# State-space parameters and x laid out on the host, loads in order of use, and TensorE in program order in the MLPs

## The chip, the cores and the metric

The kernel runs on one core of one Trainium2 chip. The metric is device time in microseconds (us); three runs of the kernel before gave 2289.91, 2291.15 and 2291.24, median 2291.15. The engines are TensorE (PE; its weight loads are PEld), VectorE (DVE), ScalarE (ACT), GpSimd (POOL) and SyncE (SP), which issues nearly all DMAs.

## The reference

A trunk of two layers over 256 tokens of width 2048, all in float32. Each layer mixes tokens in two ways at once, by differential attention (8 heads) and by a diagonal complex state-space model over 64 groups of 16 channels with 64 states each, and then runs a squared-ReLU MLP of width 8192:

```python
proj = x @ w_in[l]                      # 2048 x 4096: q, k, v, u
attn_out = diff_attention(q, k, v, lam, lam_init, attn_norm_g[l])
ssm_out = s5_mixer(u, lambda_re, lambda_im, log_dt, b_re, b_im, c_re, c_im, d, glu_w, glu_b)
mix = jnp.concatenate([attn_out, group_rms_norm(ssm_out)], axis=-1) @ w_out[l]
x = layer_norm(DEEPNORM_ALPHA * x + mix, ln1_g[l], ln1_b[l])
hid = jnp.square(jax.nn.relu(x @ w_up[l]))
x = layer_norm(DEEPNORM_ALPHA * x + hid @ w_down[l], ln2_g[l], ln2_b[l])

# s5_mixer, per group: discretize, scan over time, read out
dt = exp(log_dt); mag = exp(lr * dt); ab = mag * (cos(li * dt), sin(li * dt))
bb = f(ab, lr, li) * b                  # h[t] = ab * h[t-1] + bb @ u[t]
y = gelu(Re(c @ h) + d * u);  y = y * sigmoid(y @ glu_w + glu_b)
```

## The kernel before

Every matrix product runs in three passes on a split of both operands into a rounded part and a remainder (hi*hi, hi*lo, lo*hi), so that each weight tile that SP loads (`wfetch`, L179: 128x2x512, 512 KB, a "pair") is split by ACT (`wh`, L156) and DVE (`wl = w - wh`, L137). There are 6 buffers for raw pairs and 4 for split ones (`WS`, `WB`): the split of pair n waits until TensorE has done with pair n-4. `gemm_steps` (L216) makes one 128x512 product for both token tiles (t = 0, 1) with two accumulators `acc`; a step is one k tile of one token tile, 3 matmuls.

A layer has these stages. The mixer: eight products of 96 matmuls each from `xT` (k, u, u, q, v, v, k, q), with attention and the state-space work woven in. For the state space, `lay_params` (L356) turns the raw parameters into step factors (`ab`, `f`, powers `pw`), `base_b` and `base_c`; `half_prep` (L470) has POOL make `abc` and `fine` for half of the groups; `ssm_tables` (L489) has POOL make the table of powers in `ops` for one of eight blocks b; `ssm_turn` (L517) turns a block's `zx` on TensorE (`zT`, `pk`). Then per block: matmuls `X` (L598) from u, DVE work on `wk` with the table and a scan (L613), matmuls `Y` (L638). The two halves of X use two PSUM buffers, so the second waits until DVE has read the first. After the mixer come the output product with a layer norm (`last_chunk`), the MLP (16 blocks f: `up(f)`, 96 matmuls, then the product with `w_down` of block f-1, 96 matmuls), and a second `last_chunk`.

In the first layer x comes in rows (`load_x`), and TensorE turns it (`turn_x`, 32 transposes); the parameters come in their own layouts (`load_params`, L329, 17 DMAs) and are turned on TensorE too (L364, L365, and 16 transposes of `lc`, L246). For the second layer, `Ahead` (L554) does the state-space preparation during the first layer's MLP and spills the tables to DRAM.

What sets the order: SP's order is that of the program everywhere. In the mixer TensorE's order is fixed by a planner (`Flow`, L63): tasks wait for planned times (`L_LAY`, `L_HALF`, `L_TAB`, ...), and a step of a product advances the plan's clock by 0.68. `last_chunk` is written by hand. All else, and in the MLP TensorE as well, is put in order by the compiler's scheduler. Each engine then runs its list strictly in order.

Of the kernel before, what the change touches and what calls it, by code (L numbers as in the profile page):

```python
# [45 lines left out]
L_LOAD = 9.0  # L46
# [16 lines left out]
class Flow:  # L63
# [53 lines left out]
def trunk(ctx: ExitStack, tc: tile.TileContext, x, w_in, lambda_q1, lambda_k1, lambda_q2, lambda_k2,  # L117
          attn_norm_g, ssm_lambda_re, ssm_lambda_im, ssm_log_dt, ssm_b_re, ssm_b_im, ssm_c_re, ssm_c_im,
          ssm_d, glu_w, glu_b, ssm_norm_g, w_out, ln1_g, ln1_b, w_up, w_down, ln2_g, ln2_b, out):
# [112 lines left out]
    def gemm(*a, **kw):  # L232
        acc = {}
        for _ in gemm_steps(*a, done=acc.__setitem__, **kw):
            pass
        return acc

# [91 lines left out]
    def load_params(l):  # L329
        raw = op_tile()[0:96, 0]  # L330
        SY.dma_start(out=raw[0:32], in_=ssm_lambda_re[l].rearrange("(q g) p -> q (g p)", g=2))
        SY.dma_start(out=raw[32:64], in_=ssm_lambda_im[l].rearrange("(q g) p -> q (g p)", g=2))
        ld = ssm.tile([96, 2], F32, tag="ld", name="ld")
        SY.dma_start(out=ld[64:96], in_=ssm_log_dt[l].rearrange("(q g) -> q g", g=2))
        vec = op_tile()[0:32, 0]
        for i, v in enumerate((attn_norm_g, ssm_norm_g)):
            SY.dma_start(out=vec[8 * i:8 * i + 8], in_=v[l].rearrange("(b p) -> b p", p=P))
        for j in range(LC):
            SY.dma_start(out=vec[16:32].rearrange("x (r j c) -> x r j c", r=2, j=LC)[:, :, j],
                         in_=ssm_d[l].rearrange("(x r c) -> x r c", r=2, c=32))  # L340
# [846 lines left out]
```

## Time and profile before

| | us |
|---|---|
| median of three runs | 2291.15 |
| the profiled execution | 2289.99 |
| its span, first to last instruction | 2288.2 |
| TensorE busy | 2191.5 (96%) |
| VectorE busy | 1511.2 (66%) |
| ScalarE busy | 1080.8 (47%) |
| GpSimd busy | 341.1 (15%) |

The core's mean granted clock was 0.985. By the trace the first layer's mixer and output product run to about 475 us, its MLP to 1143, the second layer's mixer and output product to 1591, its MLP to 2236. A TensorE that is busy by the profile may still be slowed: back-to-back 128x512 matmuls start 0.227 us apart at full clock although each is shown as 0.39 us long, so the distance of starts tells more than the busy share.

### The profile page before, as it was taken

The numbers are of one execution on the slowest core, as the hardware profiler recorded it, in microseconds if no ns is written. First come the engines' busy times: TensorE is split into PE (matmuls) and PEld (weight loads), VectorE is DVE, ScalarE is ACT, GpSimd is POOL, SyncE is SP. The second block draws the span as 40 slices with busy tenths as digits, with TensorE's granted clock in tenths as the row PEclk, the third lists the DMA queues.
The fourth block names the chain that finished last, engine by engine and source line by source line (L and its number), as shares of the span: only waits on it lengthen the run. The fifth ranks groups of instructions, "written<-read, shape, count | busy, mean of one in ns | idle before, by whom it ended". The sixth has DMA issues, their size and how long they took to land.

```text
span 2288.2 us, 28955 instructions
## 1 busy us (share of the span) xinstructions
PE 2191.5 (96%) x10772; PEld 1770.5 (77%) x10772; DVE 1511.2 (66%) x1906; ACT 1080.8 (47%) x1543; POOL 341.1 (15%) x528
## 2 busy tenths in 40 slices
PE   7889889999999899999999999999999999999997
PEld 5767667788888788888877767777888888888886
DVE  5686877865765555555586996877565565556557
ACT  4445555354554445544534454544444444444443
POOL 1875500000352432310000000000000000000001
PEclk9999999999999999999999999999999999999999
DMA  7434344576566566666665654565666666666664
GB/s 221 141 111 129 107 124 149 192 206 201 177 183 203 178 203 223 204 211 209 215 215 173 201 174 133 164 220 149 185 189 187 195 186 192 191 186 190 186 198 144
DMA packets 229357, 414.35 MB, mean 181 GB/s; under 512 B 38592, under 2 KB 38752, under 8 KB 227168
## 3 DMA queue, kind: packets, MB, share of 16 engines
q1 hardware_dynamic: 228352, 405.82, 57.7%
q10 hardware_dynamic: 864, 6.69, 0.8%
q8 instruction: 85, 1.39, 0.3%
q14 instruction: 56, 0.46, 0.1%
HBM read 401.44 MB, written 11.01 MB: 180 GB/s over the span
## 4 chain that ended last, share of the span: by engine, by line
PE 75%; DVE 11%; POOL 6%; issue 4%; ACT 3%; DMA 2%; SPq 0%; DVEq 0%; ACTq 0%; POOLq 0%
PE acc L211 68%; POOL tm L137 3%; DVE wk L137 3%; DVE wl L137 3%; PE tp L246 2%; PE acc L813 2%; DVE res L153 1%; ACT wh L156 1%; POOL ops L137 1%; DVE wk L613 1%; POOL abc L137 1%; PE Y L638 1%; DVE res L137 0%; PE X L598 0%; ACT ops L156 0%
## 5 line engine op out<-in xcount | busy, mean ns | idle before, releaser
L137 DVE TENSOR_TENSOR wl<-w,wh 128x1024 fp32r<-128x1024 f32 x714 | 883.5, 1240 | 614.2 <-ACT wh L156 599.3
L156 ACT ACTIVATE wh<-w 128x1024 fp32r<-128x1024 f32 x714 | 754.0, 1060 | 802.8 <-PE acc L211 751.0
L211 PE MATMUL acc<-wh,xTh 128*128 128x512 f32 x1440 | 567.0, 401 | 7.3 <-ACT wh L156 6.7
L211 PE MATMUL acc<-wl,xTh 128*128 128x512 f32 x1440 | 567.0, 394 | 2.4 <-DVE wl L137 2.4
L211 PE MATMUL acc<-wh,xTl 128*128 128x512 f32 x1440 | 566.6, 394 | 0.0
L211 PE MATMUL acc<-wh,hidh 128*128 128x512 f32 x1024 | 407.5, 398 | 1.4 <-ACT raw L156 1.0
L211 PE MATMUL acc<-wh,hidl 128*128 128x512 f32 x1024 | 400.0, 391 | 0.0
L211 PE MATMUL acc<-wl,hidh 128*128 128x512 f32 x1024 | 399.2, 390 | 0.0
L211 PEld LDWEIGHTS acc<-wh,xTh 128*128 128x128 f32 x1440 | 274.5, 191 | 71.2 <-ACT wh L156 8.0
L211 PEld LDWEIGHTS acc<-wh,xTl 128*128 128x128 f32 x1440 | 274.2, 190 | 58.2
L211 PEld LDWEIGHTS acc<-wl,xTh 128*128 128x128 f32 x1440 | 274.5, 191 | 57.6 <-DVE wl L137 3.8
L211 PEld LDWEIGHTS acc<-wh,hidl 128*128 128x128 f32 x1024 | 192.4, 188 | 41.4
L211 PEld LDWEIGHTS acc<-wh,hidh 128*128 128x128 f32 x1024 | 192.8, 188 | 40.0 <-ACT raw L156 1.3
L211 PEld LDWEIGHTS acc<-wl,hidh 128*128 128x128 f32 x1024 | 192.8, 188 | 37.6
L137 DVE TENSOR_TENSOR res<-res,acc 128x512 f32<-128x512 f32 x288 | 196.5, 682 | 18.6 <-PE acc L211 17.0
L294 POOL TENSOR_TENSOR rs<-rs,mhalf 128x1 f32<-128x1 f32 x8 | 7.8, 978 | 1047.3 <-DVE rs L150 1047.3
L137 POOL TENSOR_TENSOR tm<-ops,pw 128x64 f32<-128x64 f32 (+2 forms) x192 | 126.1, 678 | 26.9 <-ACT ops L156 20.6
L156 ACT ACTIVATE raw<-acc 128x512 f32<-128x512 f32 x80 | 47.1, 589 | 65.2 <-PE acc L211 65.1
L137 POOL TENSOR_TENSOR ops<-tm 128x64 f32<-128x64 f32 (+2 forms) x96 | 75.6, 788 | 7.1
L150 POOL TENSOR_SCALAR ss<-ss 128x2 f32<-128x2 f32 x16 | 4.3, 269 | 394.7 <-ACT sq L156 394.7
L137 DVE TENSOR_TENSOR hidl<-tp,hidh 128x512 fp32r<-128x512 f32 x64 | 44.0, 687 | 28.7 <-ACT hidh L156 28.7
L211 PE MATMUL acc<-wh,mAh 128*128 128x512 f32 x128 | 53.6, 418 | 1.8 <-DVE res L137 1.1
(179 smaller groups left out, 1981.2 us busy)
## 6 DMA issues: line engine op xcount, KB each, us to landing
w<-in_w_up SPq DMA_DIRECT2D x256, 512.0 KB, 4.5
w<-in_w_down SPq DMA_DIRECT2D x256, 512.0 KB, 4.7
w<-in_w_in SPq DMA_DIRECT2D x128, 512.0 KB, 4.2
w<-in_w_out SPq DMA_DIRECT2D x64, 512.0 KB, 4.1
spilled<-ops SPq DMA_DIRECT2D x8, 1088.0 KB, 7.8
w<-in_glu_w SPq DMA_DIRECT2D x16, 512.0 KB, 4.1
ops<-spilled ACTq DMA_DIRECT2D x6, 1088.0 KB, 6.2
gb<-in_ln_g SPq DMA_DIRECT2D x8, 512.0 KB, 8.1
```

Source lines behind the costliest of these rows:

```text
L137: (eng or V).tensor_tensor(out=out, in0=in0, in1=in1, op=op)
L150: (eng or V).tensor_scalar(out=out, in0=a, scalar1=s1, scalar2=s2, op0=op0, **kw)
L153: V.scalar_tensor_tensor(out=out, in0=a, scalar=s, in1=b, op0=op0, op1=op1)
L156: S.activation(out=out, in_=in_, func=func, **kw)
L211: TE.matmul(out=acc, lhsT=a[:, c], rhs=b, start=(first and i == 0), stop=(last and i == 2))
L246: TE.transpose(ps[:, i], src(i), ident)
L294: G.tensor_tensor(out=self.rs, in0=self.rs, in1=mhalf[:, 0:1], op=ALU.pow)
L613: V.tensor_tensor_scan(out=flat(h[:, i]), data0=flat(dec), data1=flat(s[:, i]), initial=0.0, op0=ALU.mult, op1=ALU.add)
L638: TE.matmul(out=d, lhsT=cx[:, 2 * i + ri, 2 * hf + r].rearrange("p g c -> p (g c)"), rhs=e, start=(i == 1 and ri == 0), stop=(ri == 1), sk ...
L813: TE.matmul(out=acc[t], lhsT=(lo if i == LH else hi)[:, c], rhs=(wl if i == HL else wh)[:, k % 2], start=seen[t] == 0, stop=seen[t] == 3 * ...
```

## The change

The host now gives x a second time, by channel (`x_t`), and the state-space parameters by state and channel (`vectors`, `b_t`, `c_t`, `lambdas`). x is split from SBUF by ACT and DVE in four groups of 512 channels, without TensorE; `load_params` makes 5 DMAs instead of 17; `lay_params` has one small transpose left (`dtT`). SP's order at the start: x group 0 in two halves, two pairs, the step sizes and `vectors`, x group 1, two pairs, `b_t`, `c_t`, `lambdas`, x group 2, two pairs, x group 3, the other pairs. The rows of x (`res`) are loaded after the first q product. In the first product the token tiles alternate every 4 k tiles, where they alternated every 8. In the plan of the first mixer, two waits (`L_LOAD`, `L_LAY`) go, and `L_LAY` is put ahead of the first half on the plan's account of POOL.

In the MLPs TensorE's order is now that of the program: the transposes of block f's `raw` come after steps 4 and 9 of `up(f+1)`, and the state-space preparation of the second layer is planned by one `Flow` over the whole MLP, one block f later than before.

```diff
+    def tick(self, dt):
+
+        self.now += dt
+        t = True
+        while t:
+            t = next((t for t in self.tasks if t[2]()), None)
+            if t:
+                t[2] = next(t[1], None)
+                if t[2] is None:
+                    self.tasks.remove(t)
...
     def load_params(l):
-        raw = op_tile()[0:96, 0]
-        SY.dma_start(out=raw[0:32], in_=ssm_lambda_re[l].rearrange("(q g) p -> q (g p)", g=2))
...
+
+        ld = sm.tile([32, 2], F32, tag="ld", name="ld", bufs=1)
+        SY.dma_start(out=ld, in_=log_dt[l])
+        prm = ssm.tile([P, 96], F32, tag="prmT", name="prm")
+        SY.dma_start(out=prm, in_=vectors[l])
         yield
-        lb = ssm.tile([P, 4, NP_, GC], F32, tag="wk", name="lb")
-        for a, v in enumerate((ssm_b_re, ssm_b_im)):
...
+        wk = ssm.tile([P, 4, NP_, GC], F32, tag="wk", name="lb")
+        SY.dma_start(out=wk[:, 0:2], in_=b_t[l])
+        yield
+        base_b, base_c = (tile4k([P, 2, NP_, GC], F32, "base") for _ in range(2))
+        SY.dma_start(out=base_c, in_=c_t[l])
+        yield
         lq = ssm.tile([P, 4, HD], F32, tag="abc", name="lq")
-        for i, v in enumerate((lambda_q1, lambda_k1, lambda_q2, lambda_k2)):
-            SY.dma_start(out=lq[:, i], in_=v[l].partition_broadcast(P))
-        return raw, ld, vec, lq, lb, lc
+        SY.dma_start(out=lq.rearrange("p i d -> p (i d)"), in_=lambdas[l].partition_broadcast(P))
+        return ld, prm, lq, wk, base_b, base_c
+
+    def loading_rest(gen, to):
+        to.append((yield from gen))
...
     def lay_params(fl, p, l, loaded):
-        raw, ld, vec, lq, lb, lc = loaded
-        G.tensor_tensor(out=ld[64:96], in0=ebase[64:96, 0:2], in1=ld[64:96], op=ALU.pow)
-        V.tensor_copy(out=raw[64:96].rearrange("q (g p) -> q g p", g=2),
-                      in_=ld[64:96].unsqueeze(2).to_broadcast([32, 2, 64]))
+        ld, prm, lq, wk, base_b, base_c = loaded
+        raw = op_tile()[0:32, 0]
+        G.tensor_tensor(out=ld, in0=ebase[0:32, 0:2], in1=ld, op=ALU.pow)
+        V.tensor_copy(out=raw.rearrange("q (g p) -> q g p", g=2), in_=ld.unsqueeze(2).to_broadcast([32, 2, 64]))
+        p["vec"] = sm.tile([P, 32], F32, tag="vecT", name="vecT")
+        V.tensor_copy(out=p["vec"], in_=prm[:, 64:96])
         yield fl.slot("tp", dt=L_PARAM)
         give = fl.take("tp")
-        ps = ps_t.tile([P, 4, P], F32, tag="tp", name="prmT_ps")
-        TE.transpose(ps[:, 0, 0:96], raw, ident[0:96, 0:96])
...
+        ps = ps_t.tile([P, 4, P], F32, tag="tp", name="dtT")
+        TE.transpose(ps[:, 0, 0:32], raw, ident[0:32, 0:32])
+        dt = sm.tile([P, 32], F32, tag="dtT", name="dtT", bufs=1)
+        V.tensor_copy(out=dt, in_=ps[:, 0, 0:32])
...
-        base_b, base_c = (tile4k([P, 2, NP_, GC], F32, "base") for _ in range(2))
-        t1 = lb[:, 2:4]
...
+        lb, t1 = wk[:, 0:2], wk[:, 2:4]
+        ts(base_c[:, 1], base_c[:, 1], -1.0, ALU.mult)
...
+        fl.pool = fl.now + L_LAY
...
-            if 0 <= f - 6 < 8:
-                fl = Flow(sx=2)
-                fl.add(0, ssm_turn(fl, *self.q[f - 6][0:2]))
-                fl.run()
+            if 0 <= f - 7 < 8:
+                self.fl.add(0, ssm_turn(self.fl, *self.q[f - 7][0:2]))
...
-            if 0 <= f - 4 < 8:
-                self.q[f - 4] = ssm_tables(fl, self.p, f - 4)
+            if 0 <= f - 5 < 8:
+                self.q[f - 5] = ssm_tables(fl, self.p, f - 5)
...
-    def load_x(t, n):
-        for h in range(n):
...
+    def load_x(g):
+        xr = tile4k([P, 4, T], F32, "xr")
+        for h in range(2 if g == 0 else 1):
+            k = slice(2 * h, 2 * h + 2) if g == 0 else slice(0, 4)
+            SY.dma_start(out=xr[:, k], in_=x_t[:, 4 * g + k.start:4 * g + k.stop])
+            act(xT.hi[g][:, k], xr[:, k])
+            sub(xT.lo[g][:, k], xr[:, k], xT.hi[g][:, k].bitcast(F32))
+
+
+    loading, loaded = load_params(0), []
+    load_x(0)
+    fetched.extend([wfetch(w_in[0], k, AW) for k in (0, 2)])
+    next(loading)
+    load_x(1)
+    fetched.extend([wfetch(w_in[0], k, AW) for k in (4, 6)])
+    for _ in loading_rest(loading, loaded):
+        pass
+    load_x(2)
+    fetched.extend([wfetch(w_in[0], k, AW) for k in (8, 10)])
+    load_x(3)
+    first = lambda done: gemm_steps(xT, w_in[0], KT, AW, done)
...
-                yield lambda: loaded
-                yield fl.after(L_LOAD)
                 yield from lay_params(fl, p, 0, loaded[0])
-                yield fl.after(L_LAY)
...
-            if l == 0:
-                for i, test in enumerate(kproj(0)):
...
+            yield from kproj(0)
             for i in range(2):
                 yield from uproj(i)
             yield from qproj(0)
+            if l == 0:
+                for t in range(NT):
+                    SY.dma_start(out=res[t], in_=x[t * P:(t + 1) * P])
...
-        def up(f):
-            if f == 0:
...
+        def up(f, between=()):
+
+            acc, at = {}, dict(between)
+            steps = first(acc.__setitem__) if f == 0 else gemm_steps(xT, w_up[l], KT, f * NB, acc.__setitem__)
+            for i, _ in enumerate(steps):
+                tick()
+                if i in at:
+                    at[i]()
             hh = Split("hid", 1)
+
+            def turn(t, raw):
+                ps = transpose4(lambda i: raw[:, i * P:(i + 1) * P])
+                hh.put(t, 0, ps)
+            turns = []
             for t in range(NT):
                 raw = rawp.tile([P, NB], F32, tag="raw", name="raw")
                 act(raw, acc[t], AF.Relu)
                 act(raw, raw, AF.Square)
-                ps = transpose4(lambda i: raw[:, i * P:(i + 1) * P])
-                hh.put(t, 0, ps)
...
+                turns.append(lambda t=t, raw=raw: turn(t, raw))
+            return hh, turns
+
+        tick = lambda: None
         if l + 1 < DEPTH:
             ahead = Ahead(l + 1)
-            params = ahead.p
-        for f in range(1, NF):
...
+            params, tick = ahead.p, lambda: ahead.fl.tick(0.68)
+        with tc.manual_schedule(engines={ENG.PE}):
+            prev, turns = up(0)
+            for f in range(1, NF):
+                cur, then = up(f, ((4, turns[0]), (9, turns[1])))
+                if l + 1 < DEPTH:
+                    ahead.between(f)
+                for nb in range(4):
+                    if f == NF - 1 and 0 < nb < 3:
+                        then[nb - 1]()
+                    done = lambda t, acc: add_partial(t, acc, nb, ALPHA if f == 1 else None)
+                    for _ in gemm_steps(prev, w_down[l], 4, nb * NB, done, kt0=4 * (f - 1)):
+                        tick()
+                prev, turns = cur, then
+                if l + 1 < DEPTH:
+                    ahead.after(f)
...
+    state = lambda name: get(name).reshape(DEPTH, NP_, P).transpose(0, 2, 1)
+    column = lambda name: get(name).reshape(DEPTH, 8, P).transpose(0, 2, 1)
+    x = get("x").reshape(T, D)
+    give("x", x)
+    give("x_t", x.reshape(T, KT, P).transpose(2, 1, 0))
+    give("w_in", get("w_in"))
+    give("lambdas", np.concatenate([get("lambda_" + n) for n in ("q1", "k1", "q2", "k2")], axis=1))
+    give("log_dt", get("ssm_log_dt").reshape(DEPTH, NP_, 2))
+    skip = np.broadcast_to(get("ssm_d").reshape(DEPTH, 16, 2, 1, 32), (DEPTH, 16, 2, LC, 32))
+    give("vectors", np.concatenate([state("ssm_lambda_re"), state("ssm_lambda_im"), column("attn_norm_g"),
+                                    column("ssm_norm_g"), skip.reshape(DEPTH, 16, P).transpose(0, 2, 1)], axis=2))
+    pairs = lambda n: get(n).reshape(DEPTH, NP_, 2, *get(n).shape[2:])
+    give("b_t", np.stack([pairs("ssm_b_" + n).transpose(0, 2, 3, 1, 4).reshape(DEPTH, P, NP_, GC)
+                          for n in ("re", "im")], axis=2))
```

On TensorE, at the start of the program (`res0`, `res1` are the rows of x, `acc` the first product's accumulators; the numbers tell buffers apart). Before:

```order
L246 MATMUL tp_127<-ident_87,res0_111 128x128 x4
L246 MATMUL tp_134<-ident_87,res0_111 128x128 x4
L246 MATMUL tp_141<-ident_87,res0_111 128x128 x4
L246 MATMUL tp_148<-ident_87,res0_111 128x128 x4
L211 MATMUL acc_178<-wh_157,xTh_115 128x512
L211 MATMUL acc_178<-wl_158,xTh_115 128x512
```

The same place now, from the tenth matmul on (nothing but matmuls of `acc_168` stands ahead):

```order
L220 MATMUL acc_168<-wh_174,xTh_115 128x512
L220 MATMUL acc_168<-wl_175,xTh_115 128x512
L220 MATMUL acc_168<-wh_174,xTl_119 128x512
L362 MATMUL dtT_197<-ident_87,ops_181 128x32
L220 MATMUL acc_169<-wh_170,xTh_115 128x512
L220 MATMUL acc_169<-wl_171,xTh_115 128x512
```

The 16 transposes ahead of the first matmul are gone, and so are the 16 of the second token tile after 12 matmuls; after 12 matmuls stands the transpose of the step sizes, and the second token tile follows with the same weights.

On VectorE, during the first products, where `base_b` is made (`lb` holds the raw b and products with `f`). Before, the two `base` rows stand behind the 13th and the 14th split (`wl`) of the program:

```order
L137 TENSOR_TENSOR lb<-lb,f 128x512
L137 TENSOR_TENSOR wl<-w,wh 128x1024
L137 TENSOR_TENSOR base<-lb 128x512
L137 TENSOR_TENSOR wl<-w,wh 128x1024
L137 TENSOR_TENSOR lb<-lb,f 128x512 x2
L137 TENSOR_TENSOR base<-lb 128x512
L137 TENSOR_TENSOR wl<-w,wh 128x1024 x6
```

Now they stand behind the 10th and the 12th:

```order
L146 TENSOR_TENSOR lb<-lb,f 128x512
L146 TENSOR_TENSOR base<-lb 128x512
L146 TENSOR_TENSOR wl<-w,wh 128x1024
L146 TENSOR_TENSOR lb<-lb,f 128x512 x2
L146 TENSOR_TENSOR wl<-w,wh 128x1024
L146 TENSOR_TENSOR base<-lb 128x512
L146 TENSOR_TENSOR wl<-w,wh 128x1024 x8
```

The second `base` row, for which POOL's first half waits, moved from behind 14 splits to behind 12.

On TensorE, in the first MLP, the turn of block 4 of the second layer's state space (`zT`). Before, it stands in the midst of the product with `w_down`, between two accumulators:

```order
L211 MATMUL acc_6724<-wl_6735,hidh_6186 128x512
L211 MATMUL acc_6724<-wh_6734,hidl_6187 128x512
L525 MATMUL zT_7766<-ident_87,zx_7189 128x128 x4
L211 MATMUL acc_6725<-wh_6728,hidh_6186 128x512
L211 MATMUL acc_6725<-wl_6729,hidh_6186 128x512
```

Now:

```order
L220 MATMUL acc_7954<-wl_7959,hidh_7567 128x512
L220 MATMUL acc_7954<-wh_7958,hidl_7568 128x512
L511 MATMUL zT_7971<-ident_87,zx_7377 128x128 x4
L521 MATMUL pk_7977<-ops_7375,zx_7377 32x32 x8
L220 MATMUL acc_7954<-wh_7958,hidh_7567 128x512
L220 MATMUL acc_7954<-wl_7959,hidh_7567 128x512
```

It moved from the end of block f = 7 to the start of the product with `w_down` of f = 11, with `pk` right behind it; the other seven turns stand at the same place of their blocks.

## Rows read from the trace of the kernel before

**Rows 1.** Busy time by stretch: first MLP and second, same start and end points.

```profile
475.69:1143.03 667.34, 660.27 (x3080) 541.74 (x3079) 391.46 (x440) 322.87 (x407) 150.39 (x229) 0.99 0.65 201
1591.02:2235.55 644.53, 644.53 (x2902) 533.48 (x2901) 370.82 (x376) 298.27 (x323) 0.00 (x0) 1.00 0.63 191
```

Its columns are the stretch, its length, busy us (and instructions) of PE, PEld, DVE, ACT and POOL, the granted clock, the busy share of the DMA engines, and GB/s.

**Rows 2.** The same view of the first mixer.

```profile
0.00:51.10 51.10, 36.42 (x149) 27.25 (x150) 25.02 (x48) 18.94 (x25) 8.48 (x26) 0.93 0.75 220
74.20:100.20 26.00, 19.79 (x110) 15.60 (x108) 10.14 (x12) 10.70 (x20) 23.15 (x50) 0.94 0.51 162
116.20:318.00 201.80, 178.26 (x1165) 134.42 (x1165) 160.55 (x227) 98.57 (x219) 104.85 (x162) 0.94 0.39 117
```

**Rows 3.** PE's waits in all: for whom; us, times, longest.

```profile
PE Y L638 <- DVE wk L137: 18.5, 22, 3.2
...
PE zT L525 <- ACT zx L156: 5.7, 1, 5.7
```

**Rows 4.** PE's order of time, first matmuls: start, us, what, [idle before <-releaser].

```profile
3.88 1.09 PE L246 MATMUL tp<-ident,res 128*128 128x128 f32 x4 [3.88 <-DMA res<-in_x]
...
10.16 0.79 PE L211 MATMUL acc<-wh,xTh 128*128 128x512 f32 x1 [1.22 <-ACT wh L156]
11.42 0.80 PE L211 MATMUL acc<-wl,xTh 128*128 128x512 f32 x1 [0.46 <-DVE wl L137]
...
12.44 0.63 PE L211 MATMUL acc<-wh,xTh 128*128 128x512 f32 x1
12.87 0.63 PE L211 MATMUL acc<-wl,xTh 128*128 128x512 f32 x1
...
15.40 0.40 PE L211 MATMUL acc<-wl,xTh 128*128 128x512 f32 x1
```

**Rows 5.** The same: the wait in the first product, and its 96th matmul.

```profile
37.62 0.80 PE L211 MATMUL acc<-wh,xTh 128*128 128x512 f32 x1 [5.25 <-ACT wh L156]
...
51.11 0.39 PE L211 MATMUL acc<-wh,xTl 128*128 128x512 f32 x1
```

**Rows 6.** ACT's order of time at the start: splits that waited for their load.

```profile
9.06 1.06 ACT L156 ACTIVATE wh<-w 128x1024 fp32r<-128x1024 f32 x1 [2.10 <-DMA w<-in_w_in]
...
14.50 1.06 ACT L156 ACTIVATE wh<-w 128x1024 fp32r<-128x1024 f32 x1 [2.47 <-DMA w<-in_w_in]
```

**Rows 7.** DMA issues: count, KB each, median us from issue to landing.

```profile
lq<-in_lambda_k SPq DMA_DIRECT2D x4, 32.0 KB, 6.2
```

**Rows 8.** DVE and POOL in order of time: `base_b`, first half's start, first table's end.

```profile
62.47 0.69 DVE L137 TENSOR_TENSOR base<-lb 128x512 f32<-128x512 f32 x1
...
63.24 1.54 POOL L137 TENSOR_TENSOR tm<-base,ab 128x256 f32<-128x256 f32 x1 [1.95 <-DVE base L137]
...
66.54 1.20 POOL L137 TENSOR_TENSOR tm<-base,ab 128x256 f32<-128x256 f32 x2
...
96.90 0.72 POOL L137 TENSOR_TENSOR ops<-tm 128x256 f32<-128x256 f32 x1
```

**Rows 9.** PE in order of time: the two halves of block 0's X.

```profile
88.84 0.71 PE L598 MATMUL X<-uT,ops 64*128 64x128 f32 x8
...
98.41 1.82 PE L598 MATMUL X<-uT,ops 64*128 64x128 f32 x8 [5.86 <-DVE wk L137]
```

**Rows 10.** Chain that ended last, in order of time: pieces of both MLPs (start, us).

```profile
875.60 2.95 PE acc L211 x12
...
921.41 2.95 PE acc L211 x12
...
1657.31 40.83 PE acc L211 x180
1701.79 40.83 PE acc L211 x180
```

**Rows 11.** PE in order of time, first MLP: its two longest waits.

```profile
629.30 0.50 PE L211 MATMUL acc<-wh,hidh 128*128 128x512 f32 x1 [1.04 <-ACT raw L156]
...
793.62 1.12 PE L525 MATMUL zT<-ident,zx 128*128 128x128 f32 x4 [5.68 <-ACT zx L156]
```

More of the change, by code (lines that the diff above doesn't have):

```diff
@@ L116, in trunk @@
 @with_exitstack
-def trunk(ctx: ExitStack, tc: tile.TileContext, x, w_in, lambda_q1, lambda_k1, lambda_q2, lambda_k2,
-          attn_norm_g, ssm_lambda_re, ssm_lambda_im, ssm_log_dt, ssm_b_re, ssm_b_im, ssm_c_re, ssm_c_im,
-          ssm_d, glu_w, glu_b, ssm_norm_g, w_out, ln1_g, ln1_b, w_up, w_down, ln2_g, ln2_b, out):
+def trunk(ctx: ExitStack, tc: tile.TileContext, x, x_t, w_in, lambdas, log_dt, vectors, b_t, c_t, glu_w, glu_b,
+          w_out, ln1_g, ln1_b, w_up, w_down, ln2_g, ln2_b, out):
     nc = tc.nc
@@ L230, in gemm_steps @@
                     yield
[L232 to L236, printed above, removed]
     def split_evac(ps, hi, lo):
@@ L557, in __init__ @@
             self.loading, self.p, self.q, self.l = load_params(l), {"spilled": []}, {}, l
+            self.fl = Flow(tp=2, sx=2)
         def between(self, f):
[L561 to L564 removed]
+            if 0 <= f - 7 < 8:
+                self.fl.add(0, ssm_turn(self.fl, *self.q[f - 7][0:2]))
         def after(self, f):
[L567 removed]
+            fl = self.fl
             if f < 3:
                 try:
[L570 removed]
+                    for _ in range(2):
                         next(self.loading)
@@ L733, in trunk @@
     xT = Split("xT", 4)
-    def load_x(t, n):
-        for h in range(n):
-            cs = slice(h * D // n, (h + 1) * D // n)
-            SY.dma_start(out=res[t][:, cs], in_=x[t * P:(t + 1) * P, cs])
-    def turn_x(t):
-        for g in range(4):
-            ps = transpose4(lambda i: res[t][:, (4 * g + i) * P:(4 * g + i + 1) * P])
-            xT.put(t, 4 * g, ps)
-    load_x(0, 4)
-    turn_x(0)
-    first_w = [wpair(w_in[0], k, AW) for k in (0, 2)]
-    load_x(1, 2)
-    first_w.append(wpair(w_in[0], 4, AW))
-    loading = load_params(0)
-    first = lambda done: gemm_steps(xT, w_in[0], KT, AW, done, apart=True, pre=first_w)
+    def load_x(g):
[17 more added lines that the diff above has]
+    first = lambda done: gemm_steps(xT, w_in[0], KT, AW, done)
     NF = FF // NB
@@ L1074, in main @@
         def main():
-            if l == 0:
-                for i, test in enumerate(kproj(0)):
-                    if i == 3:
-                        with tc.manual_schedule(engines={ENG.Activation, ENG.DVE}):
-                            turn_x(1)
-                            first_w.append(wpair(w_in[0], 6, AW))
-                            fetched.extend([wfetch(w_in[0], k, AW) for k in (8, 10)])
-                        fl.now += 1.76
-                        loaded.append((yield from steps(loading, 0.0)))
-                    yield test
-            else:
-                yield from kproj(0)
+            yield from kproj(0)
             for i in range(2):
```

76 lines of the change are left out of this document (11 added, 65 removed).

## The prediction, written before the changed kernel ran

> **What bounds the kernel now.** I read the busy time by stretch first, then TensorE's waits in total, then the stretches where it waits in order of time, and the chain of waits last. The second MLP has no idle time at all: 644.53 us long, 644.53 us of TensorE. The first MLP, with the same products between the same points, takes 667.34 [rows 1]. In the first mixer TensorE idles 14.7 of the first 51.1 us and 6.2 of the 26 from 74.2 on [rows 2]. So the kernel is bound by TensorE, and there is time to be had only where it waits: the start, the first state-space blocks, the first MLP. I price these three places against the profiled execution, 2289.99 us (span 2288.2), which lies 1.2 us below the median of the runs, 2291.15. One unit first: in the second MLP a piece of 180 matmuls takes 40.83 us, so matmuls at full clock start 0.227 us apart, and a block takes 1701.79 - 1657.31 = 44.48 us [rows 10].
>
> **The start, up to the first product's 96th matmul, at 51.11 us now [rows 5].** Before, TensorE's first instruction is a transpose at 3.88, and its first matmul starts at 10.16, 1.1 us after the first pair landed (9.06) and ACT began to split it [rows 4, 6]. By 9.06, 1 MB of x and 0.5 MB of weights are in; by 14.50 four more transfers of 0.5 MB, so one takes (14.50 - 9.06) / 4 = 1.36 us [rows 6]. In the new order 0.5 MB of x stands ahead of the first pair, not 1 MB: the pair lands at 7.7, the first matmul starts at 8.8, the second, which waits for DVE's remainder, 1.26 later as now [rows 4], at 10.1. At the low clock the starts are 0.43 apart (12.44, 12.87) [rows 4].
>
> How many matmuls run at the low level? Before, 16 transposes from 3.88 on and then 11 matmuls did, until the one at 15.40 [rows 4]. Now there are no transposes ahead. At the one end 11 matmuls run low again: the 96th comes at 10.1 + 10 x 0.43 + 85 x 0.227 + 0.3 for the transpose of the step sizes = 34.0. At the other, matmuls fill the 5.6 us of the transposes (3.88 to the first matmul, less its wait) at the low level too, 13 more, so all 24 of the first four k tiles: 10.1 + 24 x 0.43 + 72 x 0.227 + 0.3 = 37.0, which is 14.1 earlier than now. The trace has one rise after transposes and fits either; I take 37.0, the nearer to what the row shows as a stretch. The Trainium skill ("TensorE: Matmul & The Clock Gate", Part 4: PE-mode transpose) says that transposes don't count as TensorE activity the way matmuls do; by it the first end would hold, and the sum below would be 3.0 lower.
>
> Do loads keep up? At 1.36 us per 0.5 MB x group 1 is in at 10.4, pair 4 (of k tiles 6 and 7) at 13.1, `b_t` and `c_t` at 15.9, x group 2 at 17.3 plus what `lambdas` costs, the last pair at 24.1 plus that. TensorE wants group 2 at 37.0 - 48 x 0.227 = 26.1, less some 3.5 for its splitting by ACT and DVE (1.06 and 1.2 for one like it, and a wait in their lists): 22.6. `lambdas` is one DMA of 128 KB repeated over partitions. By its bytes it is 0.35 us; but four DMAs of 32 KB of the same kind took up to 6.2 us from issue to landing [rows 7]. So group 2 lands between 17.6 and 23.5, against 22.6. I take no wait, since one of 128 partitions' rows in place of four is nearer to the low end. If a wait comes it is like the one at 37.62, which cost 5.25 of idle time [rows 5] and a second stretch of low clock. That wait itself stands behind the loads of the parameters, 17 DMAs, and goes with them; what is late next is the clock. The 32 transposes of x and 18 of the parameters go too; they lie ahead of the 96th matmul and are in this difference already. Range of the term: -17.1 to -9; value -14.1.
>
> **The first blocks of the state space.** X's second half waits 5.86 us at 98.41 for DVE [rows 9], which waits for POOL's first table, finished at 96.90 + 0.72 = 97.62 [rows 8]. POOL's chain from `base_b` (63.24) to that is 34.4 us [rows 8]. Counted from the 96th matmul (51.11), `base_b` is ready at +12.1 and the table at +46.5. In the new order of VectorE the second `base_b` stands behind 12 splits; the twelfth needs the eighth pair's buffers, free at the 96th matmul, and then ACT's 1.06, its own 1.2 and the 0.69 of `base_b`: +3.0. The table comes at +37.4. TensorE reaches the first half of X at 88.84 - 51.11 = +37.7 now, 3 matmuls (0.7) later in the new order, and the second half 12 matmuls and the half's 0.7 after it: +41.9. So the table is 4.5 us early, and the second half comes at +41.9 in place of 98.41 - 51.11 = +47.3: -5.4 us. That needs `ab` and `f` by then; their inputs land at 16.5 or so and the chain behind them on ACT and DVE is some 20 instructions of 0.2 to 0.4, with splits of pairs between them, so it is done well ahead of the twelfth split.
>
> What stands against it is POOL's pace: the same instruction took 1.54 us right beside DVE's splits and 0.60 each in a pair of 1.20 without [rows 8]. The Trainium skill ("SBUF — State Buffer", Who interferes with whom) says why: a VectorE instruction with two SBUF inputs, as the split is, holds a read port that GpSimd needs. In the new order POOL's 34.4 us lie beside running products, a split every 12 matmuls (2.7 us), so 12 or 13, where about 10 ran before; 3 more of 1.2 us are 3.6, and the table is then 0.9 early instead of 4.5. The sum stays, and the rival on this chain below gets more chance. Bounds: 0 (the chain gains nothing) to -7 (with the low clock behind the wait). Behind Y of block 0 the matmuls stand at the same places to within 3, and 18.5 us of waits of Y for the scan [rows 3] stay; VectorE's order differs in places, which I put at 0, -5 to +5.
>
> **The first MLP.** It is 667.34 - 644.53 = 22.8 us longer than the second [rows 1]. What must stay is eight turns: a block with one turn takes 921.41 - 875.60 = 45.81, 1.33 over 44.48 [rows 10]; eight are 10.6. One `dtT` is 0.3. The rest, 11.9 us, goes: 16 transposes of `lc` and two of the parameters (about 2.3 with the breaks), the 5.68 us wait of `zT` for ACT at 793.62 with the low clock behind it (about 7.3), the 1.04 us at 629.30, and small ones [rows 3, 11]. The long wait was for `abc`, which POOL made only just before; now `zT` of block 4 stands at f = 11, and `abc` is made behind the table of block 3 during f = 8. With `pk` and `zT` in one piece a turn may cost less than 1.33; with 0.9 each the term is -15, and if order costs waits again -8. Value -11.9.
>
> **What costs nothing.** In the second MLP the transposes move, but none goes: 0. The rows of x are 2 MB more, 4 x 1.36 = 5.4 us of DMA time, behind weights that run 6 raw pairs (16 us) ahead; uncovered it would cost 5.4. ACT and DVE split x from SBUF in place of PSUM, same sizes.
>
> **Sum.** 2289.99 - 14.1 - 5.4 - 11.9 = 2258.6; with the 1.2 us to the median 2259.8. I predict 2259, with 2249 to 2266 for this case.
>
> **Rivals.** (1) The first product waits for x or weights as it does now: 5.3 us of idle time and 16 matmuls at low clock (3.2) put the 96th at 45.5, a gain of 5.6 in place of 14.1: 2268. For it: the loads of repeated rows [rows 7]; against: 17 DMAs of parameters became 5. (2) POOL's chain holds the mixer where it is: `ab` or `c_t` come late, POOL starts at 63 as now, and the second half of X stays at 98.4. Then only the MLP gains: 2279. For it: POOL's 1.54; against: 4.5 us of lead. (3) The fixed order in the first MLP does not do what it says: the wait for `zT` only moves, and the low clock with it. Then 8 or more of the 11.9 stay: 2268 to 2271. (4) Slower: with TensorE in fixed order, each of the 30 starts of a product with `w_down` waits for ACT to empty the accumulators that `up` has just filled, since ACT has splits queued ahead; the price is the wait of 1.04 us at 629.30 [rows 11], twice a block, since both accumulators are wanted: 30 x 2 x 1.04 = 62 us, so 2322. It decides the sign from 31.4 / 30 = 1.05 us a block on. Against it: 15 such starts in the second MLP cost nothing [rows 1].
>
> **Chances.** Forecast 63 in 100, (1) 14, (2) 8, (3) 6, (4) 5, and 4 for mishaps that cancel. What a measurement of this kernel can tell from no change is about 0.2%, 4.6 us. Faster: 63 + 14 + 8 + 6 = 91; same 4; slower 5. The range goes from 2246, all three terms and VectorE's order at their far ends (-17.1, -7, -15, -5), to 2276, which takes in (1) and (3) and the near ends (-9, 0, -8, with some of VectorE's +5), and leaves out (2), (4) and the rest, 17 in 100.
>
> **What would show it.** Right: first matmul near 8.8, the 96th near 37 (34 if few matmuls run low), no wait before X's second half, the first MLP at 655 to 656 with no wait over 1.5 us and the second at 644 to 645. Wrong: an idle stretch over 3 us in the first product; X still waiting; waits for ACT at the starts of the products with `w_down`.

## The result and the profile after

The changed kernel took 2263.11 us, the median of four runs (2259.69 to 2263.16), beside 2291.19 of the kernel before: a ratio of 0.987, 95% interval 0.9853 to 0.9888. So it is faster by 28 us, 1.3%, and the whole interval lies below 1; forecast were 31.4, 2259 us. In the profiled executions the span went from 2288.2 to 2261.4, 26.8 less. Where these lie:

| stretch of TensorE | before | after | forecast | measured |
|---|---|---|---|---|
| start to the first product's 96th matmul | 51.11 | 34.14 | -14.1 | -17.0 |
| from there to X's second half of block 0 | 47.30 | 43.73 | -5.4 | -3.6 |
| from there to the last matmul with `mS` | 341.07 | 341.00 | 0 | -0.1 |
| from there to X of the second layer | 799.90 | 792.97 | -11.9 | -6.9 |
| second mixer, to its last matmul with `mS` | 315.45 | 316.04 | 0 | +0.6 |
| from there to the last matmul | 718.44 | 718.43 | 0 | 0 |

The last 15 us make the remaining 0.2. These are two executions. In the eight executions kept with this start (this one, e0, e1, e2, e5, e6, e10 and e11) the 96th matmul lies between 33.7 and 34.6 and the second mixer takes 314 to 318, so the +0.6 is scatter. The fourth stretch holds the first MLP and is called the MLP piece below. Since the transposes of `raw` moved, it begins and ends at points that both kernels share, unlike the stretch in [rows 1]. By the view of busy time, for the MLP piece and the second MLP, before (stretch, length, busy us and instructions of PE, PEld, DVE, ACT, POOL, granted clock, DMA share, GB/s):

```profile
439.48:1239.38 799.90, 789.20 (x3667) 644.55 (x3665) 488.55 (x559) 381.89 (x478) 153.38 (x232) 1.00 0.64 199
1554.83:2273.27 718.44, 716.87 (x3229) 591.52 (x3228) 428.28 (x450) 329.27 (x360) 3.13 (x3) 1.00 0.61 185
```

The same after:

```profile
418.87:1211.84 792.97, 785.28 (x3650) 643.13 (x3648) 487.51 (x552) 384.68 (x478) 152.09 (x232) 1.00 0.63 200
1527.88:2246.31 718.43, 716.88 (x3229) 591.53 (x3228) 430.67 (x450) 330.95 (x360) 3.13 (x3) 1.00 0.60 185
```

18 transposes are gone from the piece (3667 to 3650 with `dtT`), and 792.97 - 785.28 = 7.7 us of idle time are left, the largest part, 3.45, in one place. TensorE in order of time (start, us, what, idle before and its releaser):

```profile
9.15 0.80 PE L220 MATMUL acc<-wh,xTh 128*128 128x512 f32 x1 [9.15 <-ACT wh L165]
10.41 0.80 PE L220 MATMUL acc<-wl,xTh 128*128 128x512 f32 x1 [0.46 <-DVE wl L146]
...
13.99 0.62 PE L220 MATMUL acc<-wh,xTh 128*128 128x512 f32 x1
14.42 0.43 PE L220 MATMUL acc<-wl,xTh 128*128 128x512 f32 x1
...
34.14 0.39 PE L220 MATMUL acc<-wh,xTl 128*128 128x512 f32 x1
...
63.42 1.09 PE L249 MATMUL tp<-ident,uraw 128*128 128x128 f32 x8 [1.99 <-ACT uraw L165]
74.23 0.72 PE L582 MATMUL X<-uT,ops 64*128 64x128 f32 x8
77.87 0.72 PE L582 MATMUL X<-uT,ops 64*128 64x128 f32 x8
...
628.70 0.66 PE L220 MATMUL acc<-wh,hidh 128*128 128x512 f32 x1 [3.45 <-DVE res L146]
629.16 0.63 PE L220 MATMUL acc<-wl,hidh 128*128 128x512 f32 x1
```

Read against [rows 4, 5]: 11 matmuls run at the low level, most of them 0.43 apart, as before, though no transpose is ahead of them, and the wait of 5.25 is gone. Against [rows 9]: X's second half no longer waits. Against [rows 11]: the wait for `zT` is gone, but two new ones stand here, 1.99 at 63.42 and 3.45 at 628.70.

Both have one cause, and it is on another engine. ACT in order of time at the first place:

```profile
55.05 0.60 ACT L165 ACTIVATE uraw<-acc 128x512 f32<-128x512 f32 x1 [1.73 <-PE acc L220]
60.48 0.51 ACT L165 ACTIVATE ops<-fine 128x128 f32<-128x128 f32 x2 [4.83 <-POOL fine L146]
60.89 1.99 ACT L165 ACTIVATE wh<-w 128x1024 fp32r<-128x1024 f32 x2
62.79 0.58 ACT L165 ACTIVATE uraw<-acc 128x512 f32<-128x512 f32 x1
...
625.27 0.51 ACT L165 ACTIVATE ops<-fine 128x128 f32<-128x128 f32 x2 [6.80 <-POOL fine L146]
625.69 1.04 ACT L165 ACTIVATE wh<-w 128x1024 fp32r<-128x1024 f32 x1
```

VectorE at the second:

```profile
626.76 1.29 DVE L146 TENSOR_TENSOR wl<-w,wh 128x1024 fp32r<-128x1024 f32 x1 [5.56 <-ACT wh L165]
627.97 0.67 DVE L146 TENSOR_TENSOR res<-res,acc 128x512 f32<-128x512 f32 x1
```

`ssm_tables` lets ACT copy POOL's `fine` into `ops`, half a microsecond of work. The copy stands in ACT's list where POOL has not yet made its input, 4.83 and 6.80 us too early (and 6.31 at 158.57, for the other half of the groups). Behind it in the list stand weight splits and the copy of `uraw`, which have their inputs. VectorE's remainder waits for the split, the addition to `res` stands behind the remainder, TensorE waits for the accumulator, and after the wait eight matmuls start 0.43 apart (from 629.16 on). The trace calls the releaser DVE, two engines away from the cause. That POOL's late `fine` is the cause is only read from these rows so far; e1 and e5 below test it.

### The profile page after: what moved, and what is told of

Read it like the earlier page. It is cut to its first block, busy times and chain, and to the rows that moved or that the text cites. A ratio compares the mean times of both kernels' runs of the same rounds, so it can differ in the third digit from the quotient of the medians.

```text
span 2261.4 us, 28684 instructions
## 1 busy us (share of the span) xinstructions
PE 2174.3 (96%) x10706; PEld 1761.1 (78%) x10706; DVE 1507.4 (67%) x1889; ACT 1086.1 (48%) x1540; POOL 341.4 (15%) x528
## 4 chain that ended last, share of the span: by engine, by line
PE 77%; DVE 11%; POOL 4%; issue 3%; ACT 2%; DMA 2%; SPq 0%; DVEq 0%; ACTq 0%; POOLq 0%
PE acc L220 70%; DVE wk L146 3%; POOL tm L146 3%; DVE wl L146 3%; PE tp L249 2%; PE acc L800 2%; DVE res L162 1%; ACT wh L165 1%; DVE wk L597 1%; PE Y L622 1%; DMA w<-in_w_up 1%; POOL abc L146 1%; PE X L582 1%; DVE res L146 0%; POOL fine L146 0%
## 5 line engine op out<-in xcount | busy, mean ns | idle before, releaser
L220 PE MATMUL acc<-wh,xTh 128*128 128x512 f32 x1440 | 581.6, 404 | 11.6 <-ACT wh L165 9.2
L220 PE MATMUL acc<-wh,hidh 128*128 128x512 f32 x1024 | 401.0, 392 | 4.0 <-DVE res L146 3.5
L165 ACT ACTIVATE hidh<-tp 128x512 fp32r<-128x512 f32 x64 | 38.2, 598 | 99.6 <-PE tp L249 99.6
```

Source lines behind the costliest of these rows:

```text
L165: S.activation(out=out, in_=in_, func=func, **kw)
L220: TE.matmul(out=acc, lhsT=a[:, c], rhs=b, start=(first and i == 0), stop=(last and i == 2))
```

## Experiments

The runs on the first MLP together (e5 has POOL's copies in the first mixer too, the others ACT's, except e10). "Fixed" stands for three things together: TensorE in program order with the moved transposes, one `Flow`, and the preparation one block later; no run takes them apart. Every ratio is against the kernel before on the same chip, with its 95% interval; the medians come from several chips, on which the kernel before took 2289.2 to 2291.2, so rows are best compared by the piece, from one execution each, or by the ratio.

| run | MLP order | parameters | `fine` copied in the MLP by | MLP piece | us | ratio |
|---|---|---|---|---|---|---|
| before | scheduler | as stored | ACT | 799.9 | 2291.19 | 1 |
| e7 | fixed | as stored | ACT | 802.2 | 2292.69 | 1.0009 (0.9998 to 1.0020) |
| e2 | scheduler | laid out | ACT | 802.2 | 2272.41 | 0.9927 (0.9912 to 0.9942) |
| e0, changed | fixed | laid out | ACT | 793.2 | 2263.82 | 0.9881 (0.9866 to 0.9896) |
| e10 | scheduler | laid out | POOL | 793.0 | 2261.62 | 0.9875 (0.9860 to 0.9890) |
| e1 | fixed | laid out | POOL | 787.8 | 2258.03 | 0.9866 (0.9851 to 0.9880) |
| e5 | fixed | laid out | POOL | 787.6 | 2254.27 | 0.9841 (0.9826 to 0.9856) |

**e1, the copies of `fine` by POOL in the second layer's preparation.**

```diff
-        act(tab[:, :, :, 0:16], fine[:, :, hs])
+        if "spilled" in p:
+            G.tensor_copy(out=tab[:, :, :, 0:16], in_=fine[:, :, hs])
+        else:
+            act(tab[:, :, :, 0:16], fine[:, :, hs])
```

> In the second layer's tables the copies of `fine` into `ops` are made by POOL, not by ACT; nothing else changes. Theory: in the first MLP ACT's copy at 625.27 stands in its list ahead of two weight splits and waits 6.80 us for POOL; the splits, DVE's remainders and the `res` additions behind these are late, TensorE waits 3.5 us at 628.70 and then runs at 0.43 a matmul, 5.4 us in all. With the copy gone the piece from the last product with `mS` to X of the second layer goes from 792.5 to about 787, and the time from 2263.1 to 2257.5. Rival 1: VectorE itself is late by the products of `base` (some 12 us of work from 585 on): 792.5 and 2263 stay. Rival 2: the wait passes to ACT's next copies of `abc` (2.80 us at 615.29): half stays, 2260.

Measured 2258.03 (2257.68 to 2259.47). The busy time of the MLP piece:

```profile
420.19:1207.98 787.79, 783.17 (x3650) 642.47 (x3648) 486.57 (x552) 383.17 (x470) 161.16 (x240) 1.00 0.63 201
```

ACT has 8 instructions less and POOL 8 more, the piece is 5.2 shorter, and in it TensorE's longest wait is 0.82 us. The theory holds; VectorE's own work was not the cause, nor did the wait pass on. The piece shows this more clearly than the whole time: in fixed order with the new layout it took 791.3 to 793.4 in six executions with ACT's copies there (the profile after, e0, e3, e4, e6, e9) and 787.6 to 788.2 in four with POOL's (e1, e5, e8, e11).

**e5 and e11, the same in both layers.**

```diff
-        act(tab[:, :, :, 0:16], fine[:, :, hs])
+        G.tensor_copy(out=tab[:, :, :, 0:16], in_=fine[:, :, hs])
```

> POOL makes the copies of `fine` in both layers. Theory: at 60.48 ACT's copy waits 4.83 us for POOL; behind it stand two weight splits and the copy of `uraw`, and so the transposes of `uraw` at 63.42 wait 2.2 us, which is the 1.7 by which the first state-space blocks gained less than forecast. With the copy on POOL these 2.2 go too, and the time is 2 below that with the copy moved in the second layer alone: 2256. Rival: POOL's table comes later by its copy (0.5 us), X waits for it, and the 2.2 come back there: 2258.

> POOL makes the copies of `fine` in both layers, unaltered from the run before, beside the one with the zeros: 2254, with the piece from the last product with `mS` to X of the second layer at 787.

Measured 2254.27 and, in the repeat, 2254.31 (ratio 0.9845, 0.9828 to 0.9861). X's first half and second in the first of them:

```profile
72.65 0.71 PE L582 MATMUL X<-uT,ops 64*128 64x128 f32 x8
76.62 1.30 PE L582 MATMUL X<-uT,ops 64*128 64x128 f32 x8 [0.25 <-DVE wk L146]
```

The wait of 1.99 for `uraw` is gone and the second half of X comes 42.0 behind the 96th matmul (34.60), where 41.9 was forecast in the prediction. A little of the rival shows: X's second half starts 0.33 late and takes 0.58 longer, 0.9 us in all, since VectorE waits for the table (1.90 at 75.88). Against the changed kernel on the same chip (e0) one line gains 9.5 us, more than the theory's 2256 allowed. A reason shows in the busy time from 63.10 on, of the profile after and of e0:

```profile
63.10:66.60 3.50, 3.18 (x18) 2.84 (x19) 1.74 (x4) 3.50 (x9) 3.19 (x7) 1.00 0.52 161
63.10:66.60 3.50, 3.50 (x13) 3.11 (x14) 1.43 (x3) 2.57 (x7) 3.15 (x6) 0.52 0.63 186
```

The wait of 1.99 is the same in both, but in e0 the granted clock behind it was 0.52, the lower level nearly throughout, and X's second half came 45.3 behind the 96th matmul in place of 43.7; e1 and e2 were like e0, e6 like the profile after. So the held copy cost 1.7 us in some executions and 3.3 in others. The kernels of e5, e11 and e8 (below) are the fastest of the study.

**e0, the changed kernel again.**

> The changed kernel once more, unaltered, beside the others on one chip, so that they are compared with it and not with a kernel timed elsewhere. 2263 as before, with the first product's 96th matmul at 34, X's second half at 78, the last matmul with `mS` of the first mixer at 419 and X of the second layer at 1212, all to within 1.5 us.

Measured 2263.82 (2261.88 to 2264.05); 33.8, 79.2, 419.8 and 1212.9, as expected.

**e2, the layout without the fixed order.** `up`, the loop over blocks and `Ahead` are those of the kernel before:

```diff
-        with tc.manual_schedule(engines={ENG.PE}):
-            prev, turns = up(0)
-            for f in range(1, NF):
-                cur, then = up(f, ((4, turns[0]), (9, turns[1])))
+        prev = up(0)
+        for f in range(1, NF):
+            cur = up(f)
```

> The MLPs and the second layer's preparation are put in order by the scheduler, as in the kernel before; the host's layout and the start stay as changed. Theory: the fixed order and the one Flow are worth the wait for `zT` (5.7 us and the low clock behind it, about 7) but brought a wait of 5.4 at 628.70, and the 18 transposes (2.3) go by the layout alone; so the piece from the last product with `mS` to X of the second layer is 799.5 - 2.3 = 797, and the time 2263.1 + 4.7 = 2268. Rival 1: the layout carries the whole gain of the MLP, since `abc` comes earlier without the transposes of c: 792 and 2263. Rival 2: the fixed order costs more than it gives: 786 and 2257.

Measured 2272.41 (2270.74 to 2273.43), and the piece took 802.2: not the 797 of the theory, nor either rival. TensorE's two long waits in it:

```profile
619.72 0.44 PE L517 MATMUL zT<-ident,zx 128*128 128x128 f32 x2 [3.22 <-ACT ops L165]
...
775.02 0.69 PE L517 MATMUL zT<-ident,zx 128*128 128x128 f32 x2 [5.66 <-ACT zx L165]
```

The one for `abc` stays as it was in [rows 11], and one behind ACT's copy of `fine` (a wait of 4.84 on ACT at 615.13) is new. So in these executions the layout alone makes the piece 2.3 longer, in spite of 18 transposes less.

**e7, the fixed order without the layout.** The kernel before, with `up`, the loop, `Ahead` and `Flow` as changed.

```diff
-        prev = up(0)
+        with tc.manual_schedule(engines={ENG.PE}):
+            prev, turns = up(0)
```

> The kernel before with the fixed order and the one Flow in the MLPs alone; x, the parameters and the start as before, so the 18 transposes of parameters stay in the first MLP. Theory: the wait for `zT` goes here too, the 2.3 of the transposes stay, and a wait behind ACT's copy of `fine` takes 5 as in the changed kernel: the piece from the last product with `mS` to X of the second layer is 795, 4.5 below before, and the time 2286.5. Rival: the wait behind `fine` hangs on the new layout (whose parameters are ready earlier): 789, and 2281.

Measured 2292.69 (2289.32 to 2296.70, ten runs), the piece 802.2 in an execution of 2296.26. Neither theory nor rival; the whole time can't be told from that of the kernel before (the interval takes in 1). VectorE, ACT and TensorE show why nothing was gained:

```profile
549.86 0.29 DVE L148 TENSOR_TENSOR pr<-lq 128x128 f32<-128x128 f32 x1 [5.50 <-DMA lq<-in_lambda_k]
```

```profile
659.87 0.51 ACT L167 ACTIVATE ops<-fine 128x128 f32<-128x128 f32 x2 [4.39 <-POOL fine L148]
```

```profile
550.80 0.79 PE L222 MATMUL acc<-wh,hidh 128*128 128x512 f32 x1 [4.72 <-DVE res L148]
...
663.40 0.47 PE L222 MATMUL acc<-wh,xTh 128*128 128x512 f32 x1 [2.21 <-DVE res L148]
```

The wait for `zT` is gone, as in the changed kernel, but a small product of VectorE, put ahead of an addition to `res`, waits 5.50 for a load, and TensorE 4.72 behind it; ACT's copy of `fine` waits 4.39 here too, and TensorE 2.21. The first is the same pattern with a DMA in POOL's place. With the one DMA of `lambdas` for the four of `lambda_q1` to `lambda_k2`, this wait is not there in the changed kernel; whether fewer DMAs or another place in the list does it was not tried.

**e10, scheduler's order, layout, and the copies by POOL.** e2 with the line of e5.

> The MLPs put in order by the scheduler as before, the host's layout as changed, and POOL makes the copies of `fine`. With ACT's copies that order had two waits in the piece from the last product with `mS` to X of the second layer (801.8): 3.4 for ACT's list held by `fine`, 5.8 for `abc`. Theory: only the first goes, with the matmul at the low clock behind it: 797.5, against 787.1 in fixed order with the same copies, so the fixed order by itself is worth 10; time 2264 (2254.3 + 10). Rival: both waits hang on that copy, and the fixed order is worth nothing once it is gone: 788 and 2255.

Measured 2261.62 (2257.15 to 2263.11), the piece 793.0, between the two. The wait behind `fine` went, and the one for `abc` became shorter too, 5.66 to 3.23:

```profile
762.15 0.55 PE L517 MATMUL zT<-ident,zx 128*128 128x128 f32 x3 [3.23 <-ACT zx L165]
```

With the copies on POOL the fixed order is worth 793.0 - 787.6 = 5.4 us; with them on ACT 802.2 - 793.2 = 9.0.

**e3, x by rows and turned by TensorE.** Loads, turns and first product as before, five DMAs of parameters.

```diff
-    load_x(0)
-    fetched.extend([wfetch(w_in[0], k, AW) for k in (0, 2)])
+    load_x(0, 4)
+    turn_x(0)
+    first_w = [wpair(w_in[0], k, AW) for k in (0, 2)]
```

> x is loaded by rows and turned by 32 transposes on TensorE, with the order of loads and of the first product as before; the parameters stay in the host's layout (5 DMAs), and the MLPs as changed. Theory: the wait of 5.25 at 37.62 stood behind the 17 DMAs of the parameters and goes with them, with its low clock (3.2), and so do 18 small transposes (about 2): the 96th matmul comes at 51.1 - 10.4 = 40.7, against 34.1 as changed, and the time is 2263.1 + 6.6 = 2270. Rival: the wait stood behind the 2 MB of x by rows: the 96th matmul at 49, the time 2278.

Measured 2272.65 (2271.70 to 2276.41), ratio 0.9933 (0.9917 to 0.9950); the 96th matmul at 41.44, no wait at 37. The theory holds for the start; the whole is 2.6 us above its 2270, in part because X's second half came 47.2 behind the 96th matmul here. Taken in this order, 9.7 of the start's 17.0 us go with the parameters' layout (51.11 to 41.44: the wait behind their 17 DMAs, and their transposes) and 7.3 with x by channel, its order of loads and the alternation of the token tiles, which no run takes apart.

**e6, the parameters loaded late.**

```diff
+    load_x(2)
+    fetched.extend([wfetch(w_in[0], k, AW) for k in (8, 10)])
+    load_x(3)
     for _ in loading_rest(loading, loaded):
         pass
-    load_x(2)
-    fetched.extend([wfetch(w_in[0], k, AW) for k in (8, 10)])
-    load_x(3)
```

> Of the changed kernel only the order of loads is altered: `b_t`, `c_t` and `lambdas` come behind the last group of x and the 5th and 6th pair, not ahead of group 2. Theory: POOL's chain is held by the steps of `f` on ACT and VectorE, which need `vectors` alone, and not by `b_t`, so nothing is lost by their coming 5.4 us (4 x 1.36) later: 96th matmul at 34, X's second half at 78, 2263. Rival, the second of the prediction in small: POOL's start (38.84) moves 3 to 5 us, its first table ends 77 to 79 in place of 74.4, and X's second half waits for it: 81, and 2266.

Measured 2265.43 (2264.82 to 2266.65), ratio 0.9892 (0.9875 to 0.9908); 34.56 and 78.30. POOL starts at 39.35, 4.8 behind the 96th matmul as in the changed kernel (4.7), and its first table ends at 74.86 (74.44): its chain is not held by `b_t`, as the theory had it. The time is 1.6 above e0; the intervals overlap, though the four runs of each don't, and where the 1.6 come from is open. The rival's 2266 is near, its mechanism did not show.

**e4, matmuls of zeros ahead of the first product**, and **e9, transposes in their place**. One execution of each was timed, 2260.73 and 2266.11, so only the start is read from them.

```diff
+    wm = rawp.tile([P, NB], F32R, tag="raw", name="wm")
+    V.memset(wm.bitcast(F32), 0.0)
+    wacc = acc_tile()
+    for i in range(18):
+        TE.matmul(out=wacc, lhsT=wm[:, 0:P], rhs=wm, start=(i == 0), stop=(i == 17))
```

> 18 matmuls of zeros, 128x512, stand ahead of the first product, whose result nothing reads; else as changed. Before, 16 transposes and then 11 matmuls ran up to the rise of the clock; changed, no transposes and again 11. Theory: matmuls raise the clock where transposes did not; so the zeros take the low level, the first product's matmuls start 0.227 apart from the third on, and the 96th comes 9 x 0.20 = 1.8 earlier, at 32.3. Rival: the 11 at 0.43 belong to the start of the product (its operands arrive one by one), whatever ran ahead: 34.1.

> 24 transposes of zeros in place of the 18 matmuls, ahead of the first product of the changed kernel; they end at about the time of the first pair's landing. Theory: transposes don't raise the clock, so 11 matmuls of the first product start 0.43 apart as without them, and the 24th comes 8.65 us behind the first. Rival: any work on TensorE raises it: the 24th 7.4 us behind the first, as with the matmuls.

TensorE in e4 (`wm` holds the zeros):

```profile
1.43 6.22 PE L732 MATMUL acc<-wm 128*128 128x512 f32 x18 [1.43 <-DVE wm L729]
8.11 0.50 PE L220 MATMUL acc<-wh,xTh 128*128 128x512 f32 x1 [0.46 <-ACT wh L165]
...
22.11 0.49 PE L220 MATMUL acc<-wh,xTh 128*128 128x512 f32 x1 [0.72 <-ACT wh L165]
```

The zeros took the low level, and the product's matmuls ran at full clock from the first on (0.50 long in place of 0.80): the 24th came 7.45 behind the first, in place of 8.11 to 9.22 in eight runs without them. But then the fifth pair was late, since ACT split group 2 of x at 18.32, loaded a table (1.28) for `pw`, and came to the pair at 21.01; the 96th matmul started at 34.19. So the low level at the start is covered by the loads and by ACT: what it takes is waited for anyway. In e9:

```profile
1.53 5.35 PE L249 MATMUL tp<-ident,wm 128*128 128x128 f32 x24 [1.53 <-POOL half L175]
8.88 0.51 PE L220 MATMUL acc<-wh,xTh 128*128 128x512 f32 x1 [2.00 <-ACT wh L165]
10.14 0.51 PE L220 MATMUL acc<-wl,xTh 128*128 128x512 f32 x1 [0.76 <-DVE wl L146]
10.48 0.51 PE L220 MATMUL acc<-wh,xTl 128*128 128x512 f32 x1
10.79 0.63 PE L220 MATMUL acc<-wh,xTh 128*128 128x512 f32 x1
```

Neither theory: behind the transposes and 2.0 us without work, three matmuls ran at full clock (0.51 long), with a wait of 0.76 among them; then seven started 0.43 apart, and the 24th came 8.38 behind the first. The busy time of that stretch shows the level, a granted clock of 0.50 (1.2 GHz):

```profile
11.00:13.50 2.50, 2.50 (x7) 1.88 (x7) 2.47 (x4) 1.93 (x3) 0.00 (x0) 0.50 1.05 422
```

**e8, the zeros together with POOL's copies.** The edits of e4 and e5.

> POOL makes the copies of `fine` in both layers, and 18 matmuls of zeros, whose result nothing reads, stand ahead of the first product. With the zeros alone the first 24 matmuls took 7.45 us in place of 8.65, and the product then waited 0.88 and 1.03 for ACT's split of the fifth pair, so that its 96th matmul came at 34.2 as without. Theory: the loads and ACT's list set the start now, so the zeros give nothing here either: 2254, X's second half at 76.6. Rival: with other splits ahead the 1.2 to 2 us come through: 2252.

Measured 2253.59 (2253.18 to 2257.98), ratio 0.9847 (0.9833 to 0.9862), not to be told from e11 on the same chip (2254.31); the fifth pair was late again, by 1.05 at 21.98. The theory holds.

## Why the prediction was near, and where it failed

**The start: mechanism right, size off by 2.9.** The first matmul came at 9.15 (8.8 forecast), and no wait followed in that execution. The mis-sized term is the number of matmuls at the low level: I took 24, it was 11, the other end of that bound, and the 96th came at 34.14 where that end gave 34.0. That this end fits so well is partly luck, since the number is not fixed: in the eight executions with this start 7 to 13 matmuls took over 0.56 us, and the 24th came 8.11 to 9.22 behind the first. What keeps the 96th within 33.7 to 34.6 all the same is the limit that e4 showed. In e0 the first matmul came at 7.91 and 7 matmuls were slow, but TensorE then waited 0.76 at 23.19 for the fifth pair, and the 96th came at 33.83. So the first rival holds in small at this pair in e0, e1, e2, e10 and e11 (0.6 to 1.1 us each).

I had also named the Trainium skill ("TensorE: Matmul & The Clock Gate", Part 4: PE-mode transpose), by which transposes don't count the way matmuls do. Its sum came true here, but e9 differs: after 24 transposes the clock was up for three matmuls, so transposes are not nothing, as far as one execution shows. What decides how many matmuls run low is not settled.

Two readings were wrong and changed nothing. The 6.2 us of [rows 7] are a median, not the most that such a DMA took; group 2 of x landed near the low end, as ACT's split of it at 18.14 in e0 shows. And behind the wait at 37.62 six matmuls, not 16, ran at the low level before, so the first rival's price was too high.

**The first state-space blocks: 1.8 too much.** The table came 2.9 us later than forecast (POOL's start 4.7 behind the 96th matmul for 3.0, its chain 35.6 long for 34.4, with 12 splits of VectorE beside it in place of 10), and X's second half did not wait for it:

```profile
38.84 0.62 POOL L146 TENSOR_TENSOR tm<-base,ab 128x256 f32<-128x256 f32 x1 [4.10 <-DVE base L146]
...
72.69 1.75 POOL L146 TENSOR_TENSOR ops<-tm 128x256 f32<-128x256 f32 x1
```

The step that failed is the one on the first half of X, which I put only 3 matmuls later than before, at +38.4: it came 40.1 behind the 96th matmul, for the wait for `uraw` behind ACT's held copy. In e0, e1 and e2, with the low clock behind that wait, the second half comes 45.3 behind, so the term was 3.4 too large there. e5, where the copy is not held, has 42.0 for the second half.

**The first MLP: the step that failed.** I wrote that the wait of `zT` "goes", and that no wait over 1.5 us would be left. It went; a wait of 3.45 with eight matmuls at the low level took its place, 5.2 in all. It is near the third rival in its outcome (a wait goes and another comes, though 5, not 8 or more, of the 11.9 were lost), and near the fourth in kind (accumulators that are emptied late because splits stand ahead), but in one block of fifteen, and what held it was POOL. What the sum lacked is a term for ACT's list: nowhere does it ask when the copies of `fine` in it get their input from POOL. Against it stands that a turn is cheaper than I kept. The chain that ended last shows blocks without a turn and with one:

```profile
685.50 40.17 PE acc L220 x177
...
729.98 15.70 PE acc L220 x69
...
775.50 15.70 PE acc L220 x69
...
821.02 15.70 PE acc L220 x69
```

Without, 729.98 - 685.50 = 44.48; with, 821.02 - 775.50 = 45.52: 1.04 a turn in place of 1.33 [rows 10], 2.3 over eight. With both, -11.9 - 2.3 + 5.2 = -9.0; measured were -6.9. Of the 2.1 left, 1.2 are four matmuls in blocks 1, 2 and 4 (at 476.30, 521.14, 524.25 and 619.51) that start 0.2 to 0.5 late for `res`; the rest stays open. With the copies on POOL the piece is 787.8, 12.1 below before: near the forecast of -11.9 once that copy holds nobody. This nearness is luck in part: the cheaper turns (-2.3) and the 2.1 just named cancel.

My way to that sum was also wrong in one thing: I added what the layout takes away (transposes) and what the order takes away (the wait). Apart, in one execution each, they gave nothing (e2 and e7, 802.2 both). The layout alone keeps the wait for `zT` and adds one behind the copy of `fine`. The order alone takes the wait for `zT` away and adds one for the load of `lambda_k`, which the layout closes, and one behind `fine`. Together only the one behind `fine` is left.

**What was costed at nothing** cost nothing: the second MLP 718.4 in both, 2 MB more of loads without a wait.

The sum: in the profiled executions the MLP came 5.0 short, the first blocks 1.8, the second mixer 0.6, and the start gave 2.9 more: 4.5, and the median is 4.1 above 2259. That the total is so near is in part this cancelling: the three shortfalls alone are 7.4.

## What to carry to other kernels

In every list read here an engine works in order, so a small instruction can cost not its length but the lateness of its input, for all that stands behind it. When a change moves work, look in every engine's list for short copies that read what a slow engine makes late (here 0.5 us of ACT behind 20 us of POOL), and try giving such a copy to the engine that makes its input. Don't stop at the releaser that the trace names; here the cause stood two engines upstream of it. Gains of edits that move waits did not add up here; do each part alone before sharing out a sum.

## What was not expected of the hardware

In e9 the 24 transposes ran for 5.35 us, 0.21 apart, and the matmuls behind them first at full clock and only then at 1.2 GHz, for some 3 us: a rise that came late and did not last, with 2.00 and 0.76 us without work around it. The same wait of 1.99 us at 63 was followed by the lower level in e0 (granted clock 0.52) and by the full clock in the profile after (1.00); what decides is not shown. At the very start the column of the granted clock shows 1.00 (from 9.20 to 14.00 in the profile after) although matmuls start 0.43 apart; there only the distance of the starts tells the level.
